# A two-layer network on one core: expert branch behind the tenth pass, first gather in halves, down weights in 8 KB runs, twenty unread products, and two products for three in the feed-forward

## The chip, the core and the metric

The kernel runs on one core of one Trainium2 chip. The metric is the time of one execution in device microseconds, the median of the runs. The engines are TensorE (PE; its weight loads PEld), VectorE (DVE), ScalarE (ACT), GpSimd (POOL) and SyncE (SP), which issues the DMAs of the weights.

## What is computed

256 tokens of width 1024 go through two blocks of two layers, all in float32. The first block has an attention mixer and a gated feed-forward per layer; the second a mixer and a mixture of 32 experts (4 groups of 8, the best group and in it the two best experts for each token). What matters here:

```python
def conv_glu_ffn(n, w_up, conv_w, conv_b, w_down):       # D_FF = 2816
    gate, up = jnp.split(n @ w_up, 2, axis=-1)
    ...
    return (jax.nn.silu(conv) * up) @ w_down

def hier_moe(h, w_group, b_group, w_expert, b_expert, w_gate, w_up, w_down):
    ...
    for g in range(N_GROUPS):
        a = jnp.einsum('nd,edf->nef', t, w_gate[g])
        b = jnp.einsum('nd,edf->nef', t, w_up[g])
        hid = jax.nn.silu(a) * b * combine[:, g, :, None]
        y = y + jnp.einsum('nef,efd->nd', hid, w_down[g])
```

## The kernel before

The stages follow one another: `hybrid`, `ffn(0)`, `diff`, `ffn(1)`, then `mixer2(0)`, `moe(0)`, `mixer2(1)`, `moe(1)`, `final_norm`. A scheduler orders the instructions of each engine ahead of time; `issue_after` puts work behind a named instruction.

**Feed-forward** (`ffn`, L656). Float32 operands are split into a high and a low part (`split`, L234: ScalarE makes the high part at L241, VectorE the low one at L242), and a product is three: high by high, high by low, low by high (`mm3`, L276 to L278). The 2816 columns are worked on in 11 groups of 256. `up(g)` makes gate and up: for each half f of the group, for gate (`pg`) and up (`pu`), eight row blocks k with three products of 128 x 128 weights on 256 tokens, 96 products a group. One PSUM tile holds both halves of `pg` (tag `pa`), one those of `pu` (`pb`); each tag has two buffers. VectorE takes the gate out at L692 and multiplies the up part in at L703, ScalarE and POOL work in between (L696 to L702). `down(g)` (24 products of 512 columns) of one group runs beside `up` of the next.

**Experts** (`moe`, L1014). The tokens are routed on VectorE (L1051 to L1065), counted on TensorE (L1067 to L1071), and a one-hot matrix is made (L1252). Then 11 passes follow (NP = 11), each with four quarter tiles of 32 slots: experts with many tokens take more than one quarter. A gather (`gather`, L1256, products L1266) for two passes brings the tokens in as `xg`, as a product of the activations' high and low parts `nh`, `nl` with the one-hots; `nl` is a subtraction (L1041) that needs `nh` (L1047, ScalarE). `expert_pass` (L1299) multiplies `xg` with gate and up weights (L1328, 8 row blocks k by 4 quarters), makes the hidden units (L1335, L1336), transposes them (L1239), multiplies with the down weights (L1347), evicts the result as `yh`, `yl` (L260, L261) and adds it to the tokens with `scatter` (L1355).

The weights of a pass are three pieces (`piece`, L1274): gate and up of k 0 to 3, the same of k 4 to 7, and down; with three experts a piece is 3.146 MB. Pieces 3j to 3j+2 belong to pass j; each waits for a free place, and at the start of the stage six places hold pieces 0 to 5. SyncE issues them in order (L1285, and L1291 for down, two DMAs of 4 KB runs each). A pass has three experts (the last two); the one with the most tokens takes two quarters, and its number (`most`) is loaded into a register of TensorE (L1104). Tokens that find no slot would go through a general path, `overflow`, inside `tc.If` (L1169). The branch stands behind pass 3. SyncE's row there waits for the eight DMA semaphores, of all it has issued. The buffers of `yh` are shared with that path's weights (tag `yh`), so the first `yh` behind the branch waits for SyncE.

The lines named are those of the kernel before; in the changed one the unread products are L1051, the routing's counting products L1093 to L1097, the gather L1306, the issues L1330 and L1335, expert products L1381, down L1400, scatter L1408, the branch L1207, the pair of the feed-forward L694 to L697.

## Time and profile before

| | us |
|---|---|
| median of 3 runs (least, most) | 1347.06 (1345.64, 1348.57) |
| the profiled execution | 1346.1 |
| its span | 1344.2 |
| PE, DVE, ACT busy | 1213.9, 681.8, 555.1 |
| bytes moved by DMA | 335.21 MB |

A page of the profile gives busy time per engine, then the span in 40 slices, here of 33.6 us, with the rate of DMA. A window row has, behind its bounds and length, busy time and number of records of PE, PEld, DVE, ACT and POOL, then the granted clock of TensorE as a share of its full 2.4 GHz, the share of the DMA engines that was busy, and GB/s. A timeline row has the start, the time, the engine, its line, the operation, output and inputs, the shape, the number of records, and in brackets the idle time of the engine before it and what ended that; the start of `SPq` is that of SyncE's issue. In a row of a group the numbers behind the bar are busy us and mean ns of one. Matmul records overlap: what counts is the distance from start to start.

### The profile page before, as it was taken

Reading aid. Unit: us, or ns where it says so; the run is one execution under the profiler, and the core shown is the slowest. Engines: PE = TensorE matmul, PEld = TensorE weight load, DVE = VectorE, ACT = ScalarE, POOL = GpSimd, SP = SyncE. Lnnn points to the kernel's source line nnn. Section 1 sums busy time; section 2 is a strip of 40 time slices with the busy share of each in tenths; the row PEclk is TensorE's granted clock in tenths of the full one; section 3 lists DMA queues with packets and bytes.
Section 4 is the critical chain, followed back from the end, with each engine's and each line's share of the span. In section 5 each row is a group of like instructions: output and inputs, shape, how many; then the busy total and the mean of one; then the engine's idle time right before and its main releaser. Section 6 shows DMA issues by size and latency. Waiting matters only on the chain. (4 is left out here: it accounts for less than half of the span.)

```text
span 1344.2 us, 19870 instructions
## 1 busy us (share of the span) xinstructions
PE 1213.9 (90%) x7896; PEld 873.1 (65%) x7896; DVE 681.8 (51%) x1492; ACT 555.1 (41%) x994; POOL 72.9 (5%) x71
## 2 busy tenths in 40 slices
PE   7999999999999899999999798777899979949776
PEld 6867899998777799999877443233367663314332
DVE  6754755556888666556775622111166572202113
ACT  5664644444656444444675311111156632101112
POOL 0001001111000011111000000000000000000000
PEclk9999999999999999999999799889899989979988
DMA  7732455555545665551754399999996339999993
GB/s 266 251 132 93 142 184 188 188 172 177 188 142 160 228 224 184 180 181 53 287 221 175 130 408 409 360 407 409 409 386 270 142 140 358 408 363 399 409 409 142
DMA packets 144819, 335.21 MB, mean 249 GB/s; under 512 B 10448, under 2 KB 76627, under 8 KB 144723
## 3 DMA queue, kind: packets, MB, share of 16 engines
q1 hardware_dynamic: 143462, 332.94, 67.0%
q8 instruction: 65, 1.06, 0.3%
q10 hardware_dynamic: 1260, 0.95, 0.2%
q14 instruction: 32, 0.25, 0.1%
HBM read 332.82 MB, written 1.05 MB: 248 GB/s over the span
## 5 line engine op out<-in xcount | busy, mean ns | idle before, releaser
L241 ACT ACTIVATE whi<-x 128x2048 fp32r<-128x2048 f32 (+5 forms) x170 | 238.2, 1413 | 213.2 <-PE pa L277 106.0
L242 DVE TENSOR_TENSOR wlo<-x,whi 128x2048 fp32r<-128x2048 f32 (+5 forms) x166 | 277.1, 1678 | 95.8 <-ACT whi L241 88.4
L1328 PE MATMUL pa<-x,xg 128*32 128x512 f32 (+1 forms) x1408 | 179.9, 630 | 50.1 <-DVE yl L261 25.3
L276 PE MATMUL acc<-whi,big 128*128 128x512 f32 (+2 forms) x400 | 157.2, 396 | 2.6 <-ACT big L263 2.6
L277 PE MATMUL acc<-wlo,big 128*128 128x512 f32 (+2 forms) x400 | 156.0, 390 | 0.3 <-DVE wlo L242 0.3
L278 PE MATMUL acc<-whi,big 128*128 128x512 f32 (+2 forms) x400 | 154.1, 389 | 0.0
L1328 PEld LDWEIGHTS pa<-x,xg 128*32 128x32 f32 x1408 | 46.6, 115 | 151.7 <-issue 117.1
L1336 DVE SCALAR_TENSOR_TENSOR hid<-hid,cw,pa 128x128 f32<-128x128 f32 x44 | 15.1, 343 | 179.3 <-ACT hid L1335 179.3
L276 PE MATMUL pa<-big,whi 128*128 128x256 f32 x352 | 100.3, 285 | 3.7 <-DVE big L264 3.7
L276 PE MATMUL pb<-big,whi 128*128 128x256 f32 x352 | 99.8, 284 | 0.9 <-DVE rB L932 0.9
L278 PE MATMUL pa<-big,wlo 128*128 128x256 f32 x352 | 100.2, 285 | 0.0
L277 PE MATMUL pa<-big,whi 128*128 128x256 f32 x352 | 100.2, 285 | 0.0
L277 PE MATMUL pb<-big,whi 128*128 128x256 f32 x352 | 99.6, 283 | 0.0
L278 PE MATMUL pb<-big,wlo 128*128 128x256 f32 x352 | 99.6, 283 | 0.0
L1335 ACT ACTIVATE hid<-pa,cw 128x128 f32<-128x128 f32 x44 | 16.2, 367 | 195.0 <-PE pa L1328 185.8
L1347 PE MATMUL pa<-x,hidT 128*32 (+1 forms) x704 | 88.3, 620 | 5.4 <-DMA x<-in_w_down_dram 3.4
L276 PEld LDWEIGHTS acc<-whi,big 128*128 128x128 f32 x400 | 76.3, 191 | 18.6 <-ACT big L263 4.3
L278 PEld LDWEIGHTS acc<-whi,big 128*128 128x128 f32 x400 | 76.0, 190 | 15.8 <-issue 3.3
L277 PEld LDWEIGHTS acc<-wlo,big 128*128 128x128 f32 x400 | 76.4, 191 | 14.3 <-issue 1.7
L261 DVE TENSOR_TENSOR yl<-pa,yh 128x512 fp32r<-128x512 f32 x44 | 30.3, 691 | 108.4 <-ACT yh L260 108.4
L260 ACT ACTIVATE yh<-pa 128x512 fp32r<-128x512 f32 x44 | 26.2, 597 | 121.2 <-PE pa L1347 80.3
L276 PEld LDWEIGHTS pa<-big,whi 128*128 128x128 f32 x352 | 68.1, 193 | 4.9 <-issue 4.1
(350 smaller groups left out, 2201.2 us busy)
## 6 DMA issues: line engine op xcount, KB each, us to landing
x<-in_w_gate_dram SPq DMA_DIRECT2D x40, 1536.0 KB, 15.5
x<-in_w_up_dram SPq DMA_DIRECT2D x40, 1536.0 KB, 20.7
x<-in_w_down_dram SPq DMA_DIRECT2D x40, 1536.0 KB, 21.4
x<-in_ffn_w_up_dram SPq DMA_DIRECT2D x44, 1024.0 KB, 5.1
x<-in_ffn_w_down_dram SPq DMA_DIRECT2D x22, 1024.0 KB, 4.8
x<-in_w_in_dram SPq DMA_DIRECT2D x8, 1024.0 KB, 11.0
x<-in_w_out_dram SPq DMA_DIRECT2D x8, 1024.0 KB, 8.8
x<-in_hyb_w_in_dram SPq DMA_DIRECT2D x14, 512.0 KB, 6.1
```

The costliest lines, as they stand in the source:

```text
L241: self.hi = nc.scalar.activation(dst(hi), of(w), AF.Copy)
L242: self.lo = (eng or nc.vector).tensor_tensor(dst(lo), of(w), dst(hi).bitcast(F32), OP.subtract)
L260: self.hi = nc.scalar.activation(hi, psum, AF.Copy)
L261: self.lo = nc.vector.tensor_tensor(lo, psum, hi.bitcast(F32), OP.subtract)
L276: nc.tensor.matmul(out, ah, bh, start=start, stop=False)
L277: nc.tensor.matmul(out, ah, bl, start=False, stop=False)
L278: nc.tensor.matmul(out, al, bh, start=False, stop=stop)
L1328: nc.tensor.matmul(gu[s], xg[:, k, c0 + s.start:c0 + s.stop], x, start=k == 0, stop=k == KD - 1)
L1335: self.silu = nc.scalar.activation(hid, gu[:, 0, fs], AF.Silu, scale=cw[:, 1:2])
L1336: nc.vector.scalar_tensor_tensor(hid, hid, cw[:, 0:1], gu[:, 1, fs], op0=OP.mult, op1=OP.mult)
L1347: nc.tensor.matmul(pd[s], hT[f][:, s], x[:, hf * 512:hf * 512 + 512], start=f == 0, stop=f == 1)
```

## The change

In the feed-forward the high and the low part of the activations lie side by side in one tile, so that high weights by both is one product of 512 columns; low weights by high activations stays one of 256. Each f gets its own PSUM tiles, and the two halves of each are added on the way out (ScalarE copies one, VectorE adds the other). In the expert stage `nh` and `nl` of the first half are made in other places, products whose result is not read (14 behind the router's, 6 behind the counting) are added, the first gather is split, the branch is moved behind pass 9, and a down piece is one DMA whose runs are 8 KB (rows p k instead of k p, so the hidden columns are taken with a stride of 2). The router's gains are multiplied in later.

```diff
@@ ffn, up @@
+                    pg = self.ps.tile([P, 2, S], F32, name="pa")
+                    pu = self.ps.tile([P, 2, S], F32, name="pb")
                     for k0 in range(0, KD, nk):
                         for ps, (wh, wl) in zip((pg, pu), ws):
                             for k in range(k0, k0 + nk):
-                                self.mm3(ps[:, f, :], (wh[:, k, fc], wl[:, k, fc]), (nT[0][:, k, :], nT[1][:, k, :]),
-                                         start=k == 0, stop=k == KD - 1)
-                gt = pl.tile([P, 2, S], F32, name="gt")
-                nc.vector.tensor_tensor(gt, pg, rB, OP.mult)
+                                if k:
+                                    nc.tensor.matmul(ps[:, 0, :], wl[:, k, fc], nT[:, k, 0, :], start=False, stop=False)
+                                nc.tensor.matmul(ps, wh[:, k, fc], nT[:, k], start=k == 0, stop=k == KD - 1)
+                                if not k:
+                                    nc.tensor.matmul(ps[:, 0, :], wl[:, k, fc], nT[:, k, 0, :], start=False, stop=False)
+                    for dst, ps in ((gt, pg), (up, pu)):
+                        nc.scalar.activation(dst[:, f, :], ps[:, 1, :], AF.Copy)
+                        nc.vector.tensor_tensor(dst[:, f, :], dst[:, f, :], ps[:, 0, :], OP.add)
+                nc.vector.tensor_tensor(gt, gt, rB, OP.mult)
...
-                nc.vector.tensor_tensor(c, c, pu, OP.mult)
+                nc.vector.tensor_tensor(c, c, up, OP.mult)
@@ moe @@
+            def warm(n, behind):
+                x = nh[:, 0, 0:4].rearrange("p k q -> p (k q)")
+                with tc.issue_after(behind.ins):
+                    for _ in range(n):
+                        nc.tensor.matmul(idle, nh[:, 0, 0], x, start=True, stop=True)
...
-            rs = self.stats()
+            ss = self.squares()
...
+            high(0, 0)
+            rs = self.rstd(ss, D, EPS, "rs")
+            with tc.issue_after(self.exp.ins):
+                high(1, 0)
                 for tt in range(NT):
-                    nc.vector.tensor_tensor(nl[:, tt, k0:k0 + 4], hv(tt, k0), nh[:, tt, k0:k0 + 4].bitcast(F32), OP.subtract)
...
-            low(0)
+                    high(tt, 4)
+            low(0, 0)
...
+            with tc.issue_after(self.last.ins):
+                low(1, 0)
+            warm(14, routed)
             pk = self.ps.tile([P, 3, NE], F32, name="pb")
...
-            most = list(load_most(0, 1))
+            warm(6, counted)
             oh = self.one_hots(pl, s4, 0)
             with tc.issue_after(self.last.ins):
-                low(4)
+                for tt in range(NT):
+                    low(tt, 4)
...
-                    xg = self.gather(pl, oh, nh, nl, gp)
-                more = (lambda: most.extend(load_most(1, NP - 1))) if j == 0 else lambda: None
-                scatter = self.expert_pass(pl, l, j, oh, xg, idc, py, most[j] if j < NP - 1 else None, scatter, more)
+                    xg, rows = self.gather(pl, oh, nh, nl, gp)
+                    if j:
+                        rows(0, KD)
+                    else:
+                        rows(0, 4, False)
+                        with tc.issue_after(self.gathered.ins):
+                            most = list(load_most(0, 1))
+                between, more = lambda: None, lambda: None
+                if j == 0:
+                    between, more = lambda: rows(4, KD), lambda: most.extend(load_most(1, NP - 1))
...
-                if j == 3:
-                    self.prefetch(l, 0, 3 * (j + 1) + XH + XA + XB)
+                if j == NP - 2:
+                    self.prefetch(l, 0, 3 * NP)
                     with tc.If(self.most_tokens(pl, u) > 0):
                         self.overflow(pl, l, u, comb, rs, nh, nl, gp)
@@ piece @@
-                src = a["w_down_2"][l].rearrange("g e (k p) n -> p (g e) k n", p=P)
-                for i in range(2):
-                    nc.sync.dma_start(v[:, :, i], src[:, e, i])
+                src = a["w_down_2"][l].rearrange("g e (p k) n -> p (g e) (k n)", k=2)
+                nc.sync.dma_start(t.rearrange("p (e m) -> p e m", e=m), src[:, e])
@@ expert_pass @@
+            if k == 4:
+                between()
+            if k == 6 and j == 0:
+                ohT, cw = weights()
...
-            fs = slice(f * P, f * P + P)
+            x = gu.rearrange("p a (m r) -> p a r m", r=2)[:, :, f]
```

`weights()` is the block of `expert_pass` from `po` (L1309) to `cw`; it runs ahead of the products in all other passes. In `gather` the loop over k became `rows(k0, k1, both)`, with both columns of a pair evicted on ScalarE for the first half.

How the orders change, at three places. TensorE in the feed-forward, at the change from a gate block to an up block; `whi` and `wlo` are the split weights, `big` or `nT` the activations, `pa` and `pb` gate and up. Before:

```order
L276 MATMUL pa<-big_1251,whi 128x256
L277 MATMUL pa<-big_1252,whi 128x256
L278 MATMUL pa<-big_1251,wlo 128x256
L276 MATMUL pb<-big_1251,whi 128x256 [waits Activation_49]
L277 MATMUL pb<-big_1252,whi 128x256
L278 MATMUL pb<-big_1251,wlo 128x256 [waits DVE_49]
```

and now:

```order
L695 MATMUL pa<-nT,whi 128x512
L694 MATMUL pa<-nT,wlo 128x256
L695 MATMUL pa<-nT,whi 128x512
L695 MATMUL pb<-nT,whi 128x512 [waits DVE_49,Activation_49]
L697 MATMUL pb<-nT,wlo 128x256 [waits DVE_49]
L694 MATMUL pb<-nT,wlo 128x256
```

For each k two products stand where three stood, one of them twice as wide; a block of eight k is one f of one tile.

TensorE at the start of layer 0's expert stage, from the last counting product on (`mask` the choice, `oh` the one-hots, `x` the weights' places). Before:

```order
L1071 MATMUL pb<-mask,onesb 128x32
L1266 MATMUL pb<-oh,nh 128x256 [waits DVE_49,PE_49,Activation_49]
L1104 TENSOR_LOAD most [waits DVE_49]
L1104 ISA x2
L1266 MATMUL pb<-oh,nh 128x256 [waits DVE_49,Activation_49]
L1266 MATMUL pb<-oh,nl 128x256 x2
L1266 MATMUL pb<-oh,nh 128x256 x2
L1266 MATMUL pb<-oh,nl 128x256 x2
```

and now, in two pieces, the first from the last router product:

```order
L1055 MATMUL acc<-wr,hT 128x36 x3
L1051 MATMUL acc<-nh 128x512 [waits Activation_49]
L1051 MATMUL acc<-nh 128x512 x13
L1093 LDWEIGHTS belowb [waits DVE_49]
L1093 MATMUL pb<-mask,belowb 128x32 [waits PE_49]
L1094 LDWEIGHTS onesb
```

```order
L1306 MATMUL pb<-oh,nl 128x256 x2
L1306 MATMUL pb<-oh,nh 128x256 x2
L1306 MATMUL pb<-oh,nl 128x256 x2
L1130 TENSOR_LOAD most [waits DVE_49]
L1130 ISA x2
L1381 ISA
L1381 MATMUL pa<-x,xg 32x512 [waits DMAHW7_49,DMAHW0_49,Activation_49]
L1381 MATMUL pa<-x,xg 32x512 x3
```

The unread products L1051 stand behind the router's and behind the counting ones; between the first half of the gather and the first expert product only the loading of a register is left.

SyncE at the branch (`x` a place, `mi` the flag). Before, in layer 0, up to and behind the branch:

```order
L1291 DMA x<-in_w_down_dram 128x3x1024 [waits DMAHW6_49,PE_49]
L1291 DMA x<-in_w_down_dram 128x3x1024 [waits DMAHW7_49]
L1190 TENSOR_LOAD mi [waits DVE_49]
L1169 COMPARE_AND_BRANCH
```

```order
L1169 UNCONDITIONAL_BRANCH [waits DMAHW0_49,DMAHW1_49,DMAHW2_49,DMAHW3_49,DMAHW4_49,DMAHW5_49,DMAHW6_49,DMAHW7_49]
L1190 ISA x2
L1285 DMA x<-in_w_gate_dram 128x3x1024 [waits DMAHW0_49,PE_49]
L1285 DMA x<-in_w_up_dram 128x3x1024 [waits DMAHW1_49]
```

and now:

```order
L1330 DMA x<-in_w_up_dram 128x2x1024 [waits DMAHW1_49]
L1335 DMA x<-in_w_down_dram 128x2x2048 [waits DMAHW2_49,PE_49]
L1228 TENSOR_LOAD mi [waits DVE_49]
L1207 COMPARE_AND_BRANCH
```

```order
L1207 UNCONDITIONAL_BRANCH [waits DMAHW0_49,DMAHW1_49,DMAHW2_49,DMAHW3_49,DMAHW4_49,DMAHW5_49,DMAHW6_49,DMAHW7_49]
L1228 ISA x2
L230 DMA x<-in_w_in_dram 128x4x416 [waits DMAHW3_49,PE_49]
L230 DMA x<-in_w_in_dram 128x4x416 [waits DMAHW4_49]
```

Behind the row that waits for all eight semaphores the pieces of pass 5 followed; now the weights of the next mixer do, and the row ahead of the flag is the last piece of the layer, with two experts.

## Rows read from the trace of the kernel before

**Rows 1.** The page, part 2: DMA rate in 40 slices of 33.6 us.
```profile
GB/s 266 251 132 93 142 184 188 188 172 177 188 142 160 228 224 184 180 181 53 287 221 175 130 408 409 360 407 409 409 386 270 142 140 358 408 363 399 409 409 142
```

**Rows 2.** Windows and groups by form, feed-forward 0, 180 to 300 us.
```profile
180.00:300.00 120.00, 120.00 (x843) 112.33 (x843) 72.41 (x70) 55.12 (x50) 17.86 (x7) 1.00 0.54 181
...
L242 DVE TENSOR_TENSOR wlo<-x,whi 128x2048 fp32r<-128x2048 f32 x21 | 48.1, 2290 | 12.6 <-ACT whi L241 12.6
```

**Rows 3.** Timeline of PE, feed-forward and projection: start, us, operation.
```profile
318.69 0.28 PE L278 MATMUL pb<-big,wlo 128*128 128x256 f32 x1
...
319.77 0.28 PE L278 MATMUL pb<-big,wlo 128*128 128x256 f32 x1
...
319.89 0.39 PE L276 MATMUL acc<-whi,hh 128*128 128x512 f32 x1
...
320.59 0.39 PE L276 MATMUL acc<-whi,hh 128*128 128x512 f32 x1
...
738.53 0.39 PE L277 MATMUL acc<-wlo,big 128*128 128x512 f32 x1
...
739.89 0.39 PE L277 MATMUL acc<-wlo,big 128*128 128x512 f32 x1
```

**Rows 4.** Window at the start of layer 0's expert stage.
```profile
753.00:763.00 10.00, 7.09 (x29) 4.87 (x30) 8.19 (x41) 1.25 (x4) 1.25 (x5) 0.53 0.01 3
```

**Rows 5.** Timeline of DVE, PE, ACT where the expert stages start; one row of layer 1.
```profile
747.47 2.10 DVE L1041 TENSOR_TENSOR nl<-h,nh 128x512 fp32r<-128x512 f32 x2 [0.26 <-ACT nh L1047]
...
753.49 0.21 PE L1067 MATMUL pb<-mask,belowb 128*128 128x32 bf16 x1 [5.68 <-DVE mask L1065]
...
755.74 0.55 PE L1266 MATMUL pb<-oh,nh 128*128 128x256 f32 x1 [1.93 <-DVE most L1101]
...
757.12 0.63 PE L1266 MATMUL pb<-oh,nl 128*128 128x256 f32 x2
...
759.68 0.63 PE L1266 MATMUL pb<-oh,nl 128*128 128x256 f32 x2
...
765.71 6.21 PE L1328 MATMUL pa<-x,xg 128*32 128x512 f32 x54
...
758.64 0.47 ACT L1268 ACTIVATE xg<-pb,gp 128x256 f32<-128x256 f32 x1 [0.23 <-PE pb L1266]
...
1097.36 0.21 PE L1067 MATMUL pb<-mask,belowb 128*128 128x32 bf16 x1 [5.68 <-DVE mask L1065]
```

**Rows 6.** Timeline of SyncE's issues: piece 6 of either layer.
```profile
768.54 0.38 SPq L1285 DMA_DIRECT2D x<-in_w_gate_dram  x1
...
1111.13 0.37 SPq L1285 DMA_DIRECT2D x<-in_w_gate_dram  x1
```

**Rows 7.** Timeline of SyncE around the branch, layer 0, and of ACT.
```profile
839.94 7.27 SPq L1291 DMA_DIRECT2D x<-in_w_down_dram  x2
865.21 0.38 SPq L1285 DMA_DIRECT2D x<-in_w_gate_dram  x1
...
857.25 0.60 ACT L260 ACTIVATE yh<-pa 128x512 fp32r<-128x512 f32 x1 [11.13 <-SPq L1169]
```

**Rows 8.** Windows around the branch, both layers.
```profile
847.00:865.00 18.00, 11.14 (x83) 3.11 (x85) 0.98 (x2) 0.71 (x2) 0.00 (x0) 0.81 0.92 368
865.00:880.00 15.00, 13.61 (x104) 7.11 (x96) 6.01 (x17) 4.58 (x10) 0.00 (x0) 1.00 0.91 347
1180.00:1208.00 28.00, 9.71 (x74) 2.66 (x66) 1.18 (x4) 0.73 (x2) 0.00 (x0) 0.78 0.95 377
1208.00:1220.00 12.00, 10.62 (x73) 3.60 (x73) 3.20 (x11) 2.10 (x5) 0.00 (x0) 0.80 0.88 327
```

**Rows 9.** Timeline of PE, end of layer 1; of ACT, second mixer.
```profile
1297.08 5.34 PE L1328 MATMUL pa<-x,xg 128*32 x32 [4.03 <-DMA x<-in_w_up_dram]
...
1332.32 0.73 PE L1355 MATMUL acc<-yl,ohT 128*128 128x512 f32 x2
...
998.93 1.06 ACT L241 ACTIVATE whi<-x 128x1024 fp32r<-128x1024 f32 x1 [1.81 <-DMA x<-in_w_out_dram]
```

More of the change, by code (lines that the diff above doesn't have):

```diff
@@ L664, in ffn @@
             nc.scalar.dma_start(cw[3 * NF:4 * NF], a["ffn_conv_b"][l].rearrange("(f p) -> f p", p=P))
-            nT = self.prep_T(pl, self.g("ffn_norm", l))
+            nT = pl.tile([P, KD, 2, S], F32R, name="nT", bufs=1)
+            self.prep_T(pl, self.g("ffn_norm", l), parts=[nT[:, :, i, :] for i in range(2)])
             nT_split = self.hi, self.lo
@@ L1064, in moe @@
             mask = pl.tile([P, NT, NE], BF, name="mask")
[L1065 removed]
+            self.last = nc.vector.tensor_tensor(mask.rearrange("p t (r e) -> p t r e", r=4), both, grid(ohg), OP.mult)
+            with tc.issue_after(self.last.ins):
+                low(1, 0)
+            warm(14, routed)
             pk = self.ps.tile([P, 3, NE], F32, name="pb")
@@ L1070, in moe @@
             nc.tensor.matmul(pk[:, 2, :], self.onesb, mask[:, 0, :], start=True, stop=False)
-            nc.tensor.matmul(pk[:, 2, :], self.onesb, mask[:, 1, :], start=False, stop=True)
+            counted = nc.tensor.matmul(pk[:, 2, :], self.onesb, mask[:, 1, :], start=False, stop=True)
             slot, over, v, u = (pl.tile([P, NT, 3 * NP], F32, name=name) for name in ("slot", "over", "second", "u"))
@@ L1260, in gather, with rows @@
         xg = pl.tile([P, KD, m * P], F32, name="xg", tag="xg", bufs=2)
-        for k0 in range(0, KD, 2):
-            pg = self.ps.tile([P, 2, m * P], F32, name="pb")
-            for k in range(2):
-                for j, x in enumerate((nh, nl)):
-                    for tt in range(NT):
-                        nc.tensor.matmul(pg[:, k, :], x[:, tt, k0 + k, :], oh[:, tt], start=tt == 0 and j == 0,
-                                         stop=tt == 1 and j == 1)
-            nc.scalar.activation(xg[:, k0, :], pg[:, 0, :], AF.Copy, scale=gp[:, k0:k0 + 1])
-            nc.vector.tensor_scalar(xg[:, k0 + 1, :], pg[:, 1, :], gp[:, k0 + 1:k0 + 2], None, op0=OP.mult)
-        return xg
+        def rows(k0, k1, both=True):
+            for k0 in range(k0, k1, 2):
+                pg = self.ps.tile([P, 2, m * P], F32, name="pb")
+                for k in range(2):
+                    for j, x in enumerate((nh, nl)):
+                        for tt in range(NT):
+                            self.gathered = nc.tensor.matmul(pg[:, k, :], x[:, tt, k0 + k, :], oh[:, tt],
+                                                             start=tt == 0 and j == 0, stop=tt == 1 and j == 1)
+                for k in range(2):
+                    d, i, s = xg[:, k0 + k, :], pg[:, k, :], gp[:, k0 + k:k0 + k + 1]
+                    if k and both:
+                        nc.vector.tensor_scalar(d, i, s, None, op0=OP.mult)
+                    else:
+                        nc.scalar.activation(d, i, AF.Copy, scale=s)
+        return xg, rows
     def piece(self, l, n):
@@ L1297, in prefetch, with expert_pass @@
             self.piece(l, n)
-    def expert_pass(self, pl, l, j, oh, xg, idc, py, most, scatter, more):
+    def expert_pass(self, pl, l, j, oh, xg, idc, py, most, scatter, between, more):
         nc = self.nc
```

70 lines of the change are left out of this document (40 added, 30 removed).

## The prediction

> **What bounds the kernel now.** The page's slices come first [rows 1]. They show two regimes: while DMA moves 408 or 409 GB/s the weights of the experts set the pace, and elsewhere TensorE does. The windows show the second regime in the feed-forward: in 120 us TensorE is busy 120.00 at granted clock 1.00 (its level of 2.4 GHz), VectorE 72.41, ScalarE 55.12, and DMA moves 181 GB/s [rows 2]. Nothing but the products counts there. In an expert stage nothing but the DMA queue counts, and the question is when it stands still. It does so twice a layer. First at the stage's start: the six places hold the pieces of passes 0 and 1, and the queue moves 3 GB/s from 753 to 763 [rows 4] until the first products of pass 0 have freed a place; the issue of piece 6 stands at 768.54 and 1111.13 [rows 6]. Second at the branch behind pass 3: SyncE must see all its transfers land before it goes on, so its issues stop at 839.94 + 7.27 = 847.21 and begin again at 865.21 [rows 7], and the queue runs dry and refills: 368 and 347 GB/s in the first layer, 377 and 327 in the second [rows 8].
>
> **Feed-forward: three products become two.** Two layers of 11 groups with 32 triples each are 704. Today a triple is three 256-column products at (319.77 - 318.69)/9 = 0.120 us, so 0.360 [rows 3]. The new pair is one of 512 columns and one of 256. A 512-column product takes (320.59 - 319.89)/3 = 0.233 in the feed-forward's own down products and (739.89 - 738.53)/6 = 0.227 in the projection [rows 3]. The pair is 0.353 or 0.347, the saving 4.7 or 9.4 us over 704; I take the middle, 7.0. Against it: each group gets four ScalarE copies and four VectorE adds from PSUM, some 0.47 us each as the gather's eviction [rows 5]. That is 1.9 us a group on each engine, beside a group of (32 x 3 x 0.120 + 24 x 0.233) = 17.1 us in which VectorE has 72.41/7 = 10.3 and ScalarE 55.12/7 = 7.9 [rows 2]: hidden under the products of the next group. It is not hidden in the last group, where copy and add lie between the last gate and up products and the down products: 0.95 us a layer. At the start of each stage I add 0.5 us, an estimate, since the order now wants the gate products of both f ahead of their first eviction. The net is -7.0 + 1.9 + 1.0 = **-4.1**, between -7.5 and +2.9 (the last if the pair saves nothing).
>
> **Start of the expert stages.** The chain is VectorE's routing, the gather, and the products of k 0 to 3 that free place 0. Of the two subtractions that stand ahead of the logits (2.10 us for both) [rows 5] one goes behind the mask, so the mask comes 1.05 us earlier; the moved one then runs beside TensorE's counting products, of which 0.4 us was waited for anyway, and gives back 0.65. One-hots and gather start about 0.5 earlier, at 755.1 in place of 755.74. The gather's 32 products come today at (759.68 - 757.12)/12 = 0.213 us, since TensorE had stood idle for 5.68 us and was granted 0.53 [rows 4, 5]. The fourteen unread products fill 14 x 0.227 = 3.2 us of that idle stretch, the six another 1.4, and what is left idle is two gaps of about 1 us; clock 1.00 is what I take. Then the first half, 16 x 0.12, ends at about 757.4. Its evictions are on ScalarE behind two small steps that wait for the later subtractions (2.1 us of VectorE from 755.4), so the first starts near 758.0; the k 0 product can begin at 758.4, and 32 records of (6.21/54) = 0.115 us end at 762.1 [rows 5]. SyncE issues piece 6 at about 762.2: 6.3 us before 768.54. The same chain, 1097.36 - 753.49 = 343.87 us later by the first counting product in the second layer [rows 5], gives 1106.1 against 1111.13: 5.0. Piece 6 keeps the queue busy for 3.146 MB / 409 GB/s = 7.7 us, and piece 7, freed some 5.5 us behind it, comes in time. Both savings count in full, as all later pieces follow in the queue: **-11.3**. With the clock of rows 5 all the way it is 755.1 + 16 x 0.213 = 758.5 and then 32 x 0.22 = 7.0 more, 765.6: only 2.9 and 1.6, together 4.5. The unread products end near 751 and 754, ahead of the mask (752) and of the one-hots (755), so they delay neither.
>
> **Branch.** Behind the tenth pass all pieces of the layer have been issued, so the drain falls where no expert weight is behind it. The loss at its present place goes: (409 - 368)/409 x 18 + (409 - 347)/409 x 15 = 4.1 us, and (409 - 377)/409 x 28 + (409 - 327)/409 x 12 = 4.6 [rows 8], **-8.7**. What is queued behind the wait now is, in the first layer, the weights of the next mixer. These start about 4 us later against the last piece; they have a cover, since the end of the stage needs TensorE for some 15 us more, but the mixer's output weights were already 1.81 us late for ScalarE [rows 9]. I put **+1.5** there, between 0 and 4. In the second layer only the final gains are behind it. The first eviction of pass 10 waits for SyncE as that of pass 4 does today; it comes some 6 us behind the last piece and SyncE is released 2 to 3 behind it, so nothing.
>
> **End of the stage.** From the second half of pass 9 to the last scatter takes 1297.08 to 1333.05 = 36.0 us [rows 9], TensorE after piece 28's landing having all to do. The same products run there afterwards. But the branch parts pass 9 from pass 10: today the gather of pass 10 and the scatter of pass 9 fill each other's waits, and now all of pass 9 stands ahead. What that exposes is at most the gather, 32 x 0.115 = 3.7 us a layer by the smaller products' pitch, less what was slow there anyway (5.34 for 32 records that take 3.7 at 0.115) [rows 5, 9]. The bounds are -1 and +5 for both layers; I take **+1.0**, nearer to nothing since TensorE then has one long row without waits.
>
> **8 KB runs.** No row has such a run. The full slices of rows 1 lie between 399 and 409 GB/s; 2.4% of 20 pieces x 7.7 us is 3.7 us either way. The nearest row is that of the 4 KB runs, so I take **0**, and keep -3.7 and +3.7. The Trainium skill (DMA: Bandwidth & Descriptors, Bandwidth, Measured) gives, for transfers that GpSimd issues, about 10.5 ns per packet as a floor; if 8 KB runs halved the packets of the down pieces, an estimate from it is 384/16 x 10.5 ns x 20 = 5 us less, and the time would be 1320.5. No row here shows it. The router's scaling moves on VectorE beside TensorE's work: nothing.
>
> **The sum.** -4.1 - 11.3 - 8.7 + 1.5 + 1.0 + 0 = -21.6. The profiled execution took 1346.1 (span 1344.2), 1.0 below the median of the three runs, so 1324.5 there and **1325.5** as median.
>
> **Rivals.** (a) The clock isn't held: the unread products leave gaps, the gather runs at 1.2 GHz and the start gives 4.5 and not 11.3: 1332.3. For it: 5.68 us of idle were enough for 0.53; against it: gaps of about 1 us are far shorter. (b) A 512-column product costs twice one of 256, 0.240: the pair saves nothing and the feed-forward pays 2.9, so 7.0 more: 1332.5. Against it stand both 512-column pitches of rows 3. The Trainium skill (TensorE: Matmul & The Clock Gate, "Wait — 56ns, not 53.3ns?") puts only about 2.5 ns of fixed time on each product at full clock; by that the 704 products saved are worth 1.8 us, less than the 2.9 they cost, and the time would be 1330.7. The trace disagrees so far: its 256 columns take 120 ns where the page's pace is 109, and twice 0.120 less 0.227 or 0.233 leaves 7 to 13 ns that each product pays whatever its width. (c) Slower than before: the evictions of the feed-forward. A VectorE add queues behind a weight split (2.29 us for 128 x 2048 elements [rows 2]), the PSUM buffer isn't free, and TensorE waits once a group. The wait decides from 24.3/22 = 1.1 us a group on (the sum and 0.2%); with a whole split in front, 22 x 2.3 = 50.6 us, the time is 1376. For it: both engines are in order. Against it: each buffer is wanted again only after three other blocks, 3 x 8 x 0.35 = 8.4 us. (d) The drain behind pass 9 holds pass 10: if its evictions waited for SyncE like the 11.13 us that pass 4 waited [rows 7], each layer loses 9 to 11 us and the branch's gain is gone: 1345.
>
> **Numbers.** Forecast 0.56, (a) 0.16, (b) 0.13, (c) 0.06, (d) 0.06, and 0.03 for less than the range. A measurement of this kernel tells 0.2%, about 2.7 us, from no change. Faster: forecast, (a), (b), what lies below, and a third of (d), 0.90; same, half of (d), 0.03; slower 0.07, from (c) and the rest. The range: below, the pair's better pitch (-3.4), 8 KB runs (-3.7), the mixer's 1.5 and a tail of -1 instead of +1 give 1315, rounded to 1314; above, (a) or (b), 1332, with the tail's other end and 8 KB runs at theirs (5 + 3.7), 1341. Left out are (c), (d) and the corners.
>
> **What would show it.** In the profile after: the gather's products at 0.12 us with granted clock 1.00 from 747 on and piece 6 issued about 6 us earlier against the mask; 409 GB/s without the dip behind the middle of the stage, and a gap in SyncE's issues only behind piece 32; the feed-forward group near 16.8 us with TensorE busy all of it. It is wrong if TensorE idles in the feed-forward for an eviction, if the clock there is 0.5 at the gather, if the end of the stage is over 41 us long, or if down pieces take other than 7.7 us.

## The result, and the profile after

The changed kernel took 1325.36 us (median of 4 runs, 1324.14 to 1326.67), the kernel before on the same chip 1346.35 (4 runs, 1345.36 to 1348.57): a ratio of 0.984, 95% interval 0.9825 to 0.9859, against 1325.5 forecast. The profiled execution took 1325.81 with a span of 1324.0, 20.2 less than before. One execution of the kernel before, beside the later experiments, took 1506.2 us at a granted clock of 0.74 and is left out of every comparison below. The total is right, but several of the terms behind it are not, and they cancel. So the stages come first. Each is measured from VectorE's first residual add at its start to the one at its end:

| stage | before, us | after, us | difference |
|---|---|---|---|
| hybrid | 132.13 | 131.20 | -0.9 |
| feed-forward 0 | 194.99 | 192.78 | -2.2 |
| differential | 121.53 | 118.16 | -3.4 |
| feed-forward 1 | 193.69 | 191.87 | -1.8 |
| second mixer, layer 0 | 98.21 | 98.23 | 0.0 |
| expert stage 0 | 246.98 | 244.41 | -2.6 |
| second mixer, layer 1 | 96.88 | 97.69 | +0.8 |
| expert stage 1 | 247.76 | 237.80 | -10.0 |

The rest is the final norm (-0.1). Hybrid is scatter: its code is the same, and 131.1 to 133.4 occurred in the profiles of the kernels below. The second mixer of layer 1 is not: it takes 97.39 to 97.69 in every profile with the change and 96.88 and 96.94 in the two without. Why is open. The two expert stages have one program and one change, and one gained 10.0 us, the other 2.6. Cut at the issue of piece 6 and at the second half of pass 9's products they show where:

| stretch of the expert stage | layer 0, before and after | layer 1, before and after |
|---|---|---|
| residual to piece 6 | 27.99, 21.42 | 26.72, 21.78 |
| piece 6 to the second half of pass 9 | 185.55, 182.73 | 185.95, 183.15 |
| from there to the residual (end of the stage) | 33.44, 40.26 | 35.09, 32.87 |

The feed-forward, as [rows 2]: the window of 120 us, and VectorE's weight splits there by form.

```profile
177.00:297.00 120.00, 120.00 (x632) 101.91 (x631) 82.56 (x99) 64.58 (x78) 17.91 (x7) 1.00 0.55 188
...
L242 DVE TENSOR_TENSOR wlo<-x,whi 128x2048 fp32r<-128x2048 f32 x21 | 48.0, 2286 | 4.6 <-ACT whi L241 4.6
```

TensorE is still busy all of it, and no eviction holds it. VectorE went from 72.41 to 82.56 us, ScalarE from 55.12 to 64.58. GpSimd's one instruction per group gives the group's period, and the timeline of TensorE the new pair:

```profile
203.20 2.55 POOL L711 TENSOR_TENSOR c<-c,rB 128x512 f32<-128x512 f32 x1 [14.21 <-ACT c L710]
...
253.67 2.56 POOL L711 TENSOR_TENSOR c<-c,rB 128x512 f32<-128x512 f32 x1 [14.29 <-ACT c L710]
```
```profile
229.74 0.28 PE L694 MATMUL pb<-nT,wlo 128*128 128x256 f32 x1
...
231.87 0.28 PE L694 MATMUL pb<-nT,wlo 128*128 128x256 f32 x1
```

Three groups take 253.67 - 203.20, so one takes 16.82, where before (same instruction, 203.87 to 255.24) it took 17.12. The six pairs shown take 2.13, 0.355 each; the mean of the 172 pairs between 180 and 300 us is 0.350.

The start of the expert stage, as [rows 4, 5]: windows first, then timelines of TensorE and of ScalarE.

```profile
744.00:750.00 6.00, 4.03 (x31) 3.15 (x34) 5.86 (x23) 0.77 (x4) 0.41 (x2) 1.00 0.00 0
750.00:754.00 4.00, 4.00 (x36) 1.37 (x37) 2.27 (x17) 1.00 (x3) 0.86 (x3) 1.00 0.02 6
...
769.00:776.00 7.00, 7.00 (x68) 2.16 (x65) 2.37 (x8) 0.87 (x2) 0.00 (x0) 1.00 0.94 363
783.00:790.00 7.00, 7.00 (x52) 4.70 (x52) 2.63 (x5) 2.64 (x6) 0.00 (x0) 1.00 1.01 383
1112.00:1119.00 7.00, 7.00 (x64) 2.06 (x60) 2.40 (x8) 1.47 (x3) 0.00 (x0) 0.98 0.75 288
```
```profile
748.63 0.40 PE L1306 MATMUL pb<-oh,nl 128*128 128x256 f32 x2
749.96 3.64 PE L1381 MATMUL pa<-x,xg 128*32 x32 [0.93 <-ACT xg L1313]
...
762.80 0.33 PE L1277 MATMUL pb<-ident,hid 128*128 128x128 f32 x1 [2.99 <-issue]
```
```profile
749.23 0.21 ACT L1145 ACTIVATE eg<-eg 128x8 f32<-128x8 f32 x1 [6.97 <-DVE eg L1144]
...
749.45 1.55 ACT L1313 ACTIVATE xg<-pb,gp 128x256 f32<-128x256 f32 x4
```

The clock is 1.00 and the gather's products come at 0.12. But the first half of the gather ends at 749.0, and its evictions begin only at 749.45: ScalarE waits 6.97 us for `eg`, a small step that VectorE runs behind the two subtractions.

Where the start got shorter, TensorE's timeline of before shows, of which [rows 5] have the gather's first half and the 54 products at 765.71:

```profile
760.24 1.92 PE L1328 MATMUL pa<-x,xg 128*32 x2
762.09 0.62 PE L1266 MATMUL pb<-oh,nh 128*128 128x256 f32 x2
...
764.30 1.06 PE L1328 MATMUL pa<-x,xg 128*32 128x512 f32 x8
```

Two of the 32 products that free place 0 stood ahead of the gather's second half there, eight behind it, and 22 behind those. From the first of them to the issue of piece 6 it took 768.54 - 760.24 = 8.30 us, now 753.66 - 749.96 = 3.70; in layer 1 7.30 and 3.70. That is 4.6 of the 6.6 us that piece 6 gained in layer 0, and 3.6 of 4.9 in layer 1. These are readings of the two timelines; no run puts the order alone back.

SyncE's issues of pieces 6, 7 and 8:

```profile
753.66 0.38 SPq L1330 DMA_DIRECT2D x<-in_w_gate_dram  x1
...
759.88 0.37 SPq L1330 DMA_DIRECT2D x<-in_w_gate_dram  x1
...
770.03 0.37 SPq L1335 DMA_DIRECT2D x<-in_w_down_dram  x1
```

Piece 8 comes 10.2 us behind piece 7, where before it came 5.8 behind. Against the residual it isn't earlier at all: 37.79 and 39.56 us in the two layers, before 37.26 and 35.95. Its place is freed by pass 0's down products, and ahead of them TensorE spends 2.99 us on loading the counts of the later passes. A piece is 3.146 MB / 412 GB/s = 7.6 us of transfer, so the queue runs dry: 363 and 383 GB/s in layer 0, 288 in layer 1. Against 412 these three windows of 7 us lose 1.3 us in layer 0 and 2.1 in layer 1.

The branch: where the dip of [rows 8] stood the rate is now 410 to 416 GB/s. The gap in SyncE's issues stands behind the last piece (timeline of SyncE, layer 0), and at that end ScalarE shows a new wait (timeline of ScalarE; then of TensorE; then windows).

```profile
934.79 4.92 SPq L1335 DMA_DIRECT2D x<-in_w_down_dram  x1
959.71 3.65 SPq L230 DMA_DIRECT2D x<-in_w_in_dram  x4
```
```profile
955.69 0.37 ACT L1313 ACTIVATE xg<-pb,gp 128x128 f32<-128x128 f32 x1 [0.53 <-PE pb L1306]
964.45 0.90 ACT L241 ACTIVATE whi<-x 128x832 fp32r<-128x832 f32 x1 [8.40 <-DMA x<-in_w_in_dram]
965.26 0.37 ACT L1358 ACTIVATE ohT<-pb 128x256 fp32r<-128x256 f32 x1
965.52 0.89 ACT L241 ACTIVATE whi<-x 128x832 fp32r<-128x832 f32 x1
966.72 0.37 ACT L1388 ACTIVATE hid<-pa,cw 128x128 f32<-128x128 f32 x1 [0.31 <-DVE cw L1365]
...
1297.37 0.39 ACT L1358 ACTIVATE ohT<-pb 128x256 fp32r<-128x256 f32 x1
1304.41 0.37 ACT L1388 ACTIVATE hid<-pa,cw 128x128 f32<-128x128 f32 x1 [6.65 <-PE pa L1381]
```
```profile
936.39 3.64 PE L1381 MATMUL pa<-x,xg 128*32 x32 [1.07 <-DMA x<-in_w_up_dram]
...
968.01 0.48 PE L1277 MATMUL pb<-ident,hid 128*128 128x128 f32 x1 [4.92 <-DVE hid L1389]
```
```profile
951.00:958.00 7.00, 6.70 (x56) 4.70 (x58) 1.40 (x4) 1.47 (x4) 0.31 (x1) 1.00 0.68 276
958.00:965.00 7.00, 5.08 (x48) 1.30 (x40) 0.00 (x0) 0.55 (x1) 0.00 (x0) 1.00 0.59 199
```

In layer 0 the split of the next mixer's input weights stands on ScalarE ahead of pass 10's `ohT` and SiLU. Its weights are issued behind the drain, land at 964.4, and pass 10 waits 8.40 us for a matter that isn't its own. TensorE then idles 4.92 us. While the queue drains and starts again it moves 276 and 199 GB/s. In layer 1 no mixer follows, and there is no such wait. ScalarE's order before had that split behind pass 10.

Last, the page's slices of DMA rate, as [rows 1]:

```profile
GB/s 274 249 129 90 151 191 191 191 175 177 192 111 178 230 222 186 190 189 64 269 234 191 174 395 413 411 414 411 361 369 289 96 191 315 407 413 411 414 412 152
```

The full slices hold 411 to 414 where they held 407 to 409.

### The profile page after: what moved, and what is told of

Read it like the earlier page. It is cut to its first block, busy times and chain, and to the rows that moved or that the text cites. A ratio compares the mean times of both kernels' runs of the same rounds, so it can differ in the third digit from the quotient of the medians.

```text
span 1324.0 us, 18656 instructions
## 1 busy us (share of the span) xinstructions
PE 1211.9 (92%) x7232; PEld 834.0 (63%) x7232; DVE 710.7 (54%) x1576; ACT 585.8 (44%) x1086; POOL 71.3 (5%) x71
## 5 line engine op out<-in xcount | busy, mean ns | idle before, releaser
L1381 PE MATMUL pa<-x,xg 128*32 128x512 f32 (+1 forms) x1408 | 174.5, 636 | 37.1 <-DMA x<-in_w_up_dram 30.7
L695 PE MATMUL pa<-nT,whi 128*128 128x512 f32 x352 | 129.9, 404 | 3.7 <-DVE nT L264 3.7
L695 PE MATMUL pb<-nT,whi 128*128 128x512 f32 x352 | 126.7, 396 | 0.9 <-DVE rB L944 0.9
L1400 PE MATMUL pa<-x,hidT 128*32 (+1 forms) x704 | 91.6, 631 | 5.9 <-DMA x<-in_w_down_dram 4.3
L694 PE MATMUL pa<-nT,wlo 128*128 128x256 f32 x308 | 87.4, 284 | 0.0
L694 PE MATMUL pb<-nT,wlo 128*128 128x256 f32 x308 | 85.9, 279 | 0.0
L695 PEld LDWEIGHTS pa<-nT,whi 128*128 128x128 f32 x352 | 67.2, 192 | 17.9 <-issue 4.1
L695 PEld LDWEIGHTS pb<-nT,whi 128*128 128x128 f32 x352 | 65.8, 188 | 13.3 <-DVE rB L944 1.3
L276 PE MATMUL acc<-whi,hh 128*128 128x512 f32 x176 | 69.9, 397 | 0.0
L277 PE MATMUL acc<-wlo,hh 128*128 128x512 f32 x176 | 69.8, 396 | 0.0
```

What stands on the lines that cost most here:

```text
L276: nc.tensor.matmul(out, ah, bh, start=start, stop=False)
L277: nc.tensor.matmul(out, ah, bl, start=False, stop=False)
L694: nc.tensor.matmul(ps[:, 0, :], wl[:, k, fc], nT[:, k, 0, :], start=False, stop=False)
L695: nc.tensor.matmul(ps, wh[:, k, fc], nT[:, k], start=k == 0, stop=k == KD - 1)
L1381: nc.tensor.matmul(gu[s], xg[:, k, c0 + s.start:c0 + s.stop], x, start=k == 0, stop=k == KD - 1)
L1400: nc.tensor.matmul(pd[s], hT[f][:, s], x[:, hf * 512:hf * 512 + 512], start=f == 0, stop=f == 1)
```

## Experiments

The kernel before, run beside these on the same chips, took 1345.94 to 1346.32 (medians). Stages and stretches are those of the tables above, from one profile each; totals are medians. One profile places a stretch only to some 2 us: from piece 6 to pass 9 of layer 0 took 182.73 in the changed kernel, and 182.17 and 180.72 in two below whose expert stages are the same.

**Branch back behind the fourth pass** (4 runs).

```diff
-                if j == NP - 2:
-                    self.prefetch(l, 0, 3 * NP)
+                if j == 3:
+                    self.prefetch(l, 0, 3 * (j + 1) + XH + XA + XB)
```

> The changed kernel with the branch behind pass 3 again, all else as changed. Theory A: the drain costs the queue 4 to 5 us a layer where it stood, and where it stands now it costs layer 0 some 6 us, since ScalarE waits 8.40 us for the next mixer's weights ahead of pass 10's hidden units. Then from the issue of piece 6 to the products of piece 28 each layer grows by 4 to 5 us, the end of layer 0's stage shrinks from 40 us to about 34, and the whole is 2 to 4 us slower than the changed kernel (1327 to 1330). Rival B: the long end of layer 0 comes from all of pass 9 standing ahead of pass 10, not from the drain; then layer 1's end would be as long, and the whole is 9 us slower (1334), with no gain at either end.

Measured: 1325.62 (1321.52 to 1326.85), the same as the changed kernel and neither theory's total. From piece 6 to pass 9 it takes 186.16 and 185.46, so 3.4 and 2.3 us more: the drain costs that here. The windows around it:

```profile
846.00:853.00 7.00, 0.00 (x0) 0.00 (x0) 0.45 (x1) 1.08 (x3) 0.00 (x0) 0.50 0.45 177
853.00:860.00 7.00, 6.70 (x48) 1.75 (x52) 1.86 (x8) 0.28 (x2) 0.00 (x0) 0.74 0.97 356
```

But the ends take 36.2 and 30.9, less by 4.1 and 2.0. What the new place gains in the middle is lost at the end; why, the next one shows.

**The split of the next mixer's weights behind pass 10's SiLU** (4 runs).

```diff
-            self.ready = [self.split(v[:, k:k + 2]) for k in (0, 2)]
+            with self.tc.issue_after(self.silu.ins) if l else nullcontext():
+                self.ready = [self.split(v[:, k:k + 2]) for k in (0, 2)]
```

> The changed kernel with the split of the second mixer's first weights put behind the last hidden units of layer 0's experts (issue_after the last activation). Theory A: ScalarE's wait of 8.40 us for those weights ahead of pass 10 goes, the 4.92 us that TensorE stood for the hidden units go too, and the end of layer 0's stage takes about 34 to 35 us in place of 40; the whole is 4 to 6 us faster (1319 to 1321). Rival C: SyncE's release or the mixer's weights hold what follows anyway; the gain is given back in the mixer, and the whole is within 1 us.

Measured: 1319.32 (1317.03 to 1320.27), ratio to before 0.9791 (0.9771 to 0.9811), 6.0 less than the changed kernel. Expert stage 0 takes 237.70, 6.7 less; stage 1, where nothing was moved, 237.37. ScalarE at that place:

```profile
955.57 0.38 ACT L1359 ACTIVATE ohT<-pb 128x256 fp32r<-128x256 f32 x1
962.61 0.37 ACT L1389 ACTIVATE hid<-pa,cw 128x128 f32<-128x128 f32 x1 [6.65 <-PE pa L1382]
...
965.07 1.69 ACT L241 ACTIVATE whi<-x 128x832 fp32r<-128x832 f32 x2
```

`ohT` comes at 955.57, not 965.26, and the split loses nothing by standing behind. Layer 0's end takes 34.07. So 6.2 of its 6.8 us are this one place in ScalarE's order.

**The late split with the branch back** (5 runs): both edits above.

> The changed kernel with the split of the next mixer's weights behind the last pass's SiLU (as in e3, 1319.3) and the branch back behind the fourth pass (as in e1). Theory A (the branch's new place is worth its drain once the stage's end does not wait for the split): the drain returns, 3.4 us in layer 0 and 2.3 us in layer 1 from the sixth piece to the tenth pass, and nothing comes back at the ends: 1319.3 + 5.7 = 1325 us. Theory B (the place of the branch nets nothing: what the drain costs, the queue that is ahead at the end gives back): 1319 to 1320 us. Between them the two expert stages tell where: with A both are longer than e3's 237.7 and 237.4 by 3.4 and 2.3 us, with B both are within 1 us of them.

Measured: 1327.06 (1323.0 to 1329.81), ratio to before 0.9849 (0.9822 to 0.9876), 7.7 above the late split alone. Stage 0 takes 243.41, 5.7 more than there, as expected of a branch whose place is worth its drain. The order of the instructions turns out to be, on every engine, that of the first experiment: with the branch back, the split stands behind pass 10 anyway. So the two are nine runs of one order, and against the late split alone the new place is worth 6.3 to 7.7 us (1325.62 or 1327.06, less 1319.32), near the 6.2 that the prediction's terms make (-8.7 + 1.5 + 1.0). And stage 1, 242.98 here and 237.74 there, differs by 5.2 without any change. The end explains most of this. TensorE's first products there and the windows from pass 9's second half on, of the first experiment and of this one:

```profile
1280.58 4.95 PE L1381 MATMUL pa<-x,xg 128*32 x32 [4.04 <-DMA x<-in_w_up_dram]
```
```profile
1280.00:1300.00 20.00, 17.86 (x136) 8.20 (x137) 4.33 (x14) 3.78 (x9) 0.00 (x0) 0.92 1.02 413
```
```profile
1280.71 6.34 PE L1382 MATMUL pa<-x,xg 128*32 x32 [4.07 <-DMA x<-in_w_up_dram]
```
```profile
1280.00:1300.00 20.00, 17.72 (x99) 8.20 (x100) 3.53 (x9) 3.25 (x8) 0.00 (x0) 0.67 1.02 415
```

With a granted clock of 0.92 the end took 30.9, with 0.67 it took 35.4. So one profile's end can't price a branch in layer 1, and the -2.2 there in the second table can't be put down to the change: the clock of its first 21 us was 0.76 before and 0.92 after.

**Without the unread products** (4 runs).

```diff
-            warm(14, routed)
...
-            warm(6, counted)
```

> The changed kernel without the twenty unread products. Theory: they keep the granted clock at 1.00; without them the first half of the gather and the products of k 0 to 3 run at half the clock, piece 6 is issued 3 to 4 us later in each layer, and the whole is 6 to 8 us slower (1331 to 1333). Rival: the order (first half first, subtraction moved) gives the gain and the clock little, since evictions on ScalarE set the pace: piece 6 less than 1.5 us later, whole at most 2 us slower.

Measured: 1324.37 (1323.5 to 1327.53), 1.0 less than the changed kernel, which the runs don't tell from nothing. The clock did fall, to 0.50 (its level of 1.2 GHz), and the gather's first half did run at 0.213 a product. The windows of the gather and of the queue behind it:

```profile
744.00:750.00 6.00, 2.53 (x15) 2.46 (x16) 5.76 (x20) 0.00 (x0) 0.24 (x1) 0.50 0.02 1
...
769.00:776.00 7.00, 7.00 (x70) 2.16 (x66) 2.40 (x8) 0.87 (x2) 0.00 (x0) 1.00 1.01 410
783.00:790.00 7.00, 7.00 (x52) 4.70 (x52) 2.66 (x6) 2.58 (x6) 0.00 (x0) 1.00 1.02 407
```

Still piece 6 is issued 21.58 and 21.94 us behind the residual, against 21.42 and 21.78. The first half of the gather ends some 1.1 us later, but in the changed kernel TensorE waits about that long for the evictions, which wait for ScalarE's small steps. And the 32 products behind it run at clock 1.00 in both, 3.64 us. The clock was not what the start gained. Behind piece 6 the kernel without them is even ahead: piece 8 comes 1.1 and 2.5 us earlier (36.71 and 37.08 behind the residual), and the queue stays at 410 and 407 where the changed kernel had 363 and 383. VectorE's order came out otherwise: the second half of pass 0's hidden units stands ahead of the copy of the first, so TensorE gets both at once; in the changed kernel it stands behind the copy, and two down products, 1.42 us long, part the two transposes.

**Evictions first** (4 runs): the two subtractions of `low(tt, 4)` go behind the small steps.

```diff
-            with tc.issue_after(self.last.ins):
-                for tt in range(NT):
-                    low(tt, 4)
...
-            nc.vector.tensor_tensor(ew[:, 0], m2, m1, OP.subtract)
+            with tc.issue_after(nc.vector.tensor_tensor(ew[:, 0], m2, m1, OP.subtract).ins):
+                for tt in range(NT):
+                    low(tt, 4)
```

> The changed kernel with the later half's subtractions on VectorE (2.2 us) put behind the two small steps that ScalarE waits for ahead of the gather's evictions. Theory D: these evictions, not the clock, set when place 0 comes free, so the first one starts as soon as its gather products are done, piece 6 is issued 1.2 to 1.6 us earlier in each layer. The whole gains 0 to 3 us, less than that where the queue then waits for piece 8 instead. Rival: TensorE's products are the limit, piece 6 comes less than 0.5 us earlier.

Measured: 1324.55 (1320.98 to 1326.15). Piece 6 comes 1.0 us earlier in both layers (20.41 and 20.77), a little less than theory D's 1.2 to 1.6, which the total can't tell. **The same without the unread products** (4 runs):

> As the run before (evictions first), but without the twenty unread products. Theory D: now that the evictions don't wait, the clock is what is left, the gather's first half takes 3.4 us and not 2.1 and piece 6 is issued 1 to 2 us later than with the unread products. Rival: the clock is back before it counts, and piece 6 comes within 0.5 us.

Measured: 1326.06 (1324.44 to 1328.4), piece 6 at 22.91 and 22.33, 2.5 and 1.6 us later than with them. Once the evictions no longer wait, the slow gather is what ends last, and the unread products save time at piece 6; the totals are too close to show it.

**4 KB runs again** (4 runs): the down pieces in two DMAs, with the same layout in the place.

```diff
-                src = a["w_down_2"][l].rearrange("g e (p k) n -> p (g e) (k n)", k=2)
-                nc.sync.dma_start(t.rearrange("p (e m) -> p e m", e=m), src[:, e])
+                src = a["w_down_2"][l].rearrange("g e (p k) n -> p (g e) k n", k=2)
+                for i in range(2):
+                    nc.sync.dma_start(v[:, :, i], src[:, e, i])
```

> The changed kernel with each down piece as two DMAs of 4 KB runs, same rows in the same places. Theory: 8 KB runs make a down piece some 3% faster (windows of 7 us with most of a down piece show 417 to 424 GB/s, others 405 to 410), worth 0.23 us for each of 20 pieces: piece 6 to piece 28 grows by 1.5 to 2 us a layer and the whole by 3 to 4 us (1328 to 1329). Rival: the higher windows come from something else (mean rate the same), change under 1 us.

Measured: 1329.17 (1328.04 to 1332.06), 3.8 more than the changed kernel. Its slices, from the page:

```profile
GB/s 262 248 128 95 159 191 191 191 175 174 195 109 179 236 224 184 185 189 61 278 226 189 186 391 408 409 409 409 364 371 285 96 191 322 409 408 408 409 409 156
```

The full ones are back at 408 and 409, so the 8 KB runs give about 1% on the whole queue. The stretch that was to grow by 1.5 to 2 us a layer doesn't show it: piece 6 to pass 9 took 183.82 and 182.23, 1.1 more and 0.9 less, within what one profile tells. The price stands on the totals and the rate.

**The feed-forward of before** (4 runs): its three products and no evictions.

```diff
-                                if k:
-                                    nc.tensor.matmul(ps[:, 0, :], wl[:, k, fc], nT[:, k, 0, :], start=False, stop=False)
-                                nc.tensor.matmul(ps, wh[:, k, fc], nT[:, k], start=k == 0, stop=k == KD - 1)
...
+                                self.mm3(ps[:, f, :], (wh[:, k, fc], wl[:, k, fc]), (nT[0][:, k, :], nT[1][:, k, :]),
+                                         start=k == 0, stop=k == KD - 1)
...
```

> The changed kernel with the feed-forward of the kernel before (three products of 256 columns, one PSUM tile for both halves). Theory: the two products for three are worth 0.31 us a group (17.12 against 16.81) less the eviction in the last group, 2 us a layer: the feed-forward stages take 2 us more each, the whole 4 us more (1329 to 1330). Rival: part of the 4 us that the stages lost came from something else that moved (start of the stage, splits of the next stage), then less than 2 us.

Measured: 1331.22 (1328.87 to 1331.94), 5.9 more, above the 4 expected. The two stages take 2.2 and 1.8 us more, as they did before; of the rest, 1.9 stand in expert stage 1 of its profile, where nothing was changed.

**The router's scaling at once** (4 runs): layer 0's scaling goes back to its load, in the changed kernel.

```diff
-            if l == 0:
-                with self.tc.issue_after(self.lo.ins):
-                    self.scale_router()
...
+        if l == 0:
+            self.scale_router()
```

> The changed kernel with the first layer's router gains multiplied in where the router is loaded, as before the change. Theory: that step on VectorE, 2.63 us long behind its DMA, stands between two steps of the attention before, holds the normalisation of the last heads and lets TensorE idle and then run at half the clock; the attention stage takes 3 us more, the whole 3 us more (1328 to 1329). Rival: the 3.4 us that this stage lost between the two profiles have another cause, and the whole changes by less than 1 us.

**The kernel before with that scaling later** (10 runs): it alone goes behind the split of the attention output.

```diff
+            if l == 0:
+                with self.tc.issue_after(self.lo.ins):
+                    self.scale_router()
...
```

> The kernel before with one edit alone: layer 0's scaling of the router's weights (2.63 us on VectorE at 437.08, ahead of the attention output's low part) goes behind the split of that output, as in the changed kernel. Theory A (that step is what the differential stage lost, 3.4 us): its residual comes 3 us earlier against the first feed-forward stage, total about 1343 us. Theory B (the stage was shortened by something else, such as the feed-forward stage that came before leaving its weights earlier; e6, with the scaling at once, kept the shorter stage): no change, 1346 us.

Measured: 1324.74 (1324.34 to 1325.1) and 1344.60 (1342.24 to 1345.99). In the second the differential stage is 118.20 long, 3.3 us shorter than before, and the span 3.2 less; the median is 1.3 less, ratio 0.9994 (0.9977 to 1.001), so the total does not separate it from nothing. The first keeps the short stage although the step is back. The step in the kernel before, with TensorE's wait behind it, then the step in the first of these and TensorE's wait in the second:

```profile
437.08 2.63 DVE L1011 TENSOR_TENSOR wr<-wr,gains 128x288 f32<-128x288 f32 x1 [0.72 <-DMA wr<-in_w_group_dram]
...
443.51 0.68 PE L649 MATMUL pb<-ident,o 128*128 128x128 f32 x4 [2.31 <-DVE o L643]
```
```profile
434.51 0.51 DVE L1021 TENSOR_TENSOR wr<-wr,gains 128x288 f32<-128x288 f32 x1 [0.48 <-DMA wr<-in_w_group_dram]
```
```profile
441.74 0.68 PE L649 MATMUL pb<-ident,o 128*128 128x128 f32 x4 [0.47 <-DVE o L643]
```

The same instruction takes 2.63 us in one and 0.51 in the other. Where it is long it holds the copy of the attention output behind it: TensorE idles 2.31 us in place of 0.47, and the output projection behind that runs at a granted clock of 0.82 and 0.61 (443 to 446 and 446 to 449 us) in place of 1.00. Together the stage is 3.3 us longer; where the step is short or elsewhere, nothing. Why it was long stays open: GpSimd was working on a weight split in both profiles.

**Three together** (5 runs): late split, evictions first, and the loads of the counts behind pass 0's down products. **And without the unread products** (5 runs).

```diff
...
-        more()
...
+        with self.tc.issue_after(down.ins):
+            more()
```

> The changed kernel with three things together: the late split (e3: -6.0 us), the first gather's evictions ahead of the second half's low parts (e7: the sixth piece 1.0 us earlier in each layer), and the loads of the counts for the later passes behind the down products of the first pass, not ahead of them. If the three add, 1319.3 - 2 x 1.0 - up to 2 x 1.5 (half of the 2.99 us that TensorE spends on those loads) = 1314 to 1317 us, with the eighth piece less late behind the seventh than the 10.2 and 11.6 us of the changed kernel. Rival: what comes earlier at the start is waited for again when the queue has run dry, so that only the late split counts: 1318 to 1320 us.

> The same without the twenty products that nothing reads. If they matter only once evictions no longer set the pace (e7 against e8: the sixth piece 2.5 and 1.6 us later without them), this is 2 to 4 us above the run with the three together. Rival: that lateness is made up behind the sixth piece, since the queue is dry there anyway: within 1 us of it.

Measured: 1312.61 (1312.03 to 1315.45), ratio to before 0.9756 (0.973 to 0.9782), and 1315.90 (1315.24 to 1317.12), 0.9779 (0.9754 to 0.9804). The first beats both kernels, and is 1.4 below the range expected; its stages take 233.95 and 236.11. TensorE's wait ahead of pass 0's down products is down from 2.99 to 1.07 us, and the queue is full where it was dry (timeline of TensorE; windows):

```profile
760.52 0.33 PE L1275 MATMUL pb<-ident,hid 128*128 128x128 f32 x1 [1.07 <-DVE hid L1386]
```
```profile
769.00:776.00 7.00, 7.00 (x56) 1.89 (x48) 0.63 (x5) 0.00 (x0) 0.00 (x0) 0.76 1.02 417
783.00:790.00 7.00, 7.00 (x52) 4.65 (x52) 2.63 (x5) 2.83 (x6) 0.00 (x0) 1.00 1.03 408
```

Here piece 6 to pass 9 takes 180.73 and 180.82 us, about 2 less than in the changed kernel; one profile can't price that closer than the 1.3 and 2.1 us that the windows there lost. Piece 6 comes 1.1 and 1.7 us earlier with the unread products than without, and they are worth 3.3 us by the medians; the two intervals of the ratio overlap, but four of the five runs with them are below all five without.

## Why the prediction was right, and where it was not

**Feed-forward, -4.1: right, in its parts too.** The stages gave 2.2 + 1.8 = 4.0. A group is 0.30 us shorter (17.12 - 16.82), 9.4 ns for each of 32 pairs: between the two pitches worked out from [rows 3] (6.7 and 13.4 ns), 6.6 us over 22 groups where 7.0 was taken. It came in another way, though: in the mean from start to start the 512-column product takes 0.234, no better than the slower pitch, and the 256-column one beside it 0.116, not 0.120. So the ends of the stages paid 2.6 where 2.9 were put. The 2.5 ns of the Trainium skill (TensorE: Matmul & The Clock Gate, "Wait — 56ns, not 53.3ns?") would have saved 1.8 in all; here the measurement decides against it. Rival (b) falls with the pair at 0.350, and with the 2.2 and 1.8 us that the feed-forward of before brought back; rival (c) with 120.00 busy in 120.

**Start of the expert stages, -11.3: right in size, wrong in its cause.** Piece 6 comes 6.6 and 4.9 us earlier against the residual, where 6.3 and 5.0 were worked out. The step that fails is "clock 1.00 is what I take", as the thing that decides, and with it the price of rival (a), 4.5. Without the unread products the clock is 0.50 and piece 6 comes as early. The working itself had the evictions behind the small steps (758.0, the gather at 757.4), and that wait is the one that ended last, so it covers the slow gather; and the 32 products ran in 3.64, where (a) had put 7.0. The reading behind that price fails too: of the 32 products of before's gather only the first sixteen came at 0.213, the second sixteen, but for two, at 0.12 (762.54 to 763.97). What the timelines show in the clock's place is the order: the 32 products no longer have the gather's second half between them.

**"Both savings count in full": half wrong.** Pieces 6 and 7 came in time. Piece 8 came late, since the loads of the counts stand ahead of the down products that free its place; the order that VectorE got with the unread products delays it too. The queue ran dry, for 1.3 and 2.1 us in the windows shown. With the loads moved and the evictions first the same windows of layer 0 are full.

**Branch, -8.7, with +1.5 for the next mixer and +1.0 for the end.** The drain alone is worth 5.7 by the first experiment's middles (3.4 + 2.3), and the place 6.3 to 7.7 by the totals with the late split. By rates, as the -8.7 was worked out, the first experiment's two windows still lose 4.9 us in layer 0, against 412 GB/s: so not all that the queue loses there is missed at the end of the stretch. Why is open. In layer 1 any cost of the place at the end can't be told from the clock's. In layer 0 the step that fails is the +1.5 with its bounds of 0 and 4, together with the +1.0 between -1 and +5: 6.8 us came back there, and the late split removed 6.0 to 6.7 of it. The cover named was TensorE's 15 us; but the late weights are split on ScalarE, in order, ahead of pass 10's own two steps, where before, and with the branch back, that split stood behind them. Rival (d) had pass 10 held by the drain, for the wrong reason (the eviction's wait for SyncE): what held it, in one layer, was the load issued behind the drain.

**8 KB runs, 0: wrong by 3.8, at the edge of its bounds.** The -3.7 of the range is what they gave. The estimate of -5 from the packet floor of the Trainium skill (DMA: Bandwidth & Descriptors, Bandwidth, Measured) is nearer than 0, though that figure is for transfers that GpSimd issues, and these are SyncE's. The number of packets fell from 144819 to 136270.

**The router's scaling, "nothing": wrong by 3.3 in the profile.** The term was put at nothing without a row. The step stood on VectorE ahead of a copy that the output projection waits for, and took 2.63 us there, as the trace of before already showed.

**The sum.** -4.0, -11.5 at the start, -5.6 in the middle (the drain and the longer runs, less the dry queue), +4.6 at the two ends, -3.4 in the differential stage and -0.2 in the rest make -20.1, but for rounding the 20.2 of the spans. The two terms that were not counted on, -3.8 and -3.4, stood against the two that failed, 6 us at layer 0's end and some 3 of the dry queue. The right total is partly luck. (The range's upper end adds the tail's 5 to a sum that holds 1.0 of it already; added up rightly it is 1340, not 1341.)

## What to carry to other kernels

When a transfer is made later, ask which engine consumes it first and what stands behind that consumer on its in-order queue: an early split of a late weight held ScalarE, and another pass behind it, for 8.40 us, and putting it behind that pass gave 6.0. When a start is made earlier, follow each of the next pieces, not the first alone, since each is freed by another step. And a filler product for the clock was worth something here only once no other wait ended later: measure it with that wait gone.

## What was not expected of the hardware

Down runs of 8 KB in place of 4 KB raised the full rate from 409 to about 412 GB/s, 3.8 us here by the totals. One VectorE instruction of 128 x 288 elements took 2.63 us in one kernel and 0.51 in another; what stretched it is open. The end of the second expert stage took 30.9 or 35.4 us with one and the same order of instructions, as the granted clock of its first 20 us was 0.92 or 0.67; TensorE had waited 4.04 and 4.07 us for a transfer just before it in both.
